# First two modulation vectors taken in four quarters of features, with the first three column blocks of the input projection fed from each quarter

## The chip, the cores and the metric

The kernel runs on one core of one Trainium2 chip. A core has five engines that run side by side and wait for each other through semaphores: TensorE (PE in the profile, its weight loads PEld), VectorE (DVE), ScalarE (ACT), GpSimd (POOL) and SyncE (SP). Here SP issues nearly all transfers; sixteen DMA engines carry them. The metric is the device time of one launch in microseconds.

## The reference, cut to what matters

Two transformer blocks over 256 tokens of 2048 features, all in float32. Only the start of the first block matters here. Six modulation vectors come from the condition `c`; the first two of them scale and shift the normalized input, and the result `h` is multiplied with `w_in` (2048 x 8192), whose columns are the state space input (1024), queries, keys and values (1024 each) and two gates (2048 each).

```python
mod = silu(c) @ w_ada[l] + b_ada[l]                 # 12288 values
sh1, sc1, g1, sh2, sc2, g2 = split(mod, 6)
h = rms_norm(x, norm_mix_g[l]) * (1.0 + sc1) + sh1  # 256 x 2048
z = h @ w_in[l]                                     # 256 x 8192
```

The state space branch takes the first 1024 columns of `z`. Before it can start it needs tables that depend only on its parameters (decay, angle, cosines and sines of 128 steps, block diagonal input and output operands). Attention with a relative position bias takes queries, keys and values. The merged branches, a feed forward, and a second block with its own mixer and an expert layer follow; none of that is touched.

## The kernel before

**Layout.** Activations lie feature major: 128 features on the partitions, 256 tokens along the row, 16 chunks for 2048 features. A product is taken with weights as the stationary operand (128x128) and a chunk of `h` as the moving one (128x256), summed in PSUM over the 16 chunks. For accuracy each operand is split in two parts, `hi` (rounded by ScalarE) and `lo` (the rest, by VectorE), and three products are summed: hi x hi, hi x lo, lo x hi. A block of 512 columns is 192 products in two PSUM banks.

**Weights.** `piece` loads 512 rows of 512 columns (1 MiB) into a tile `w` of pool tag W (4 buffers), ScalarE writes `wh` (tag H, 2 buffers) and VectorE `wl` (tag L, 2 buffers). `gemm` takes four pieces for one block; after each quarter of a piece's products it calls `bg`.

**Background work.** Everything that isn't on the main path is a Python generator in the list `work`. Each step issues some instructions and yields its VectorE time as the writer of the kernel reckoned it, the credit. `bg(dve, ada)` adds `dve` credits and issues steps, one generator after the other, until they are used up (at most 3 are carried over). `ada` moves the list `stream`, from which the later modulation vectors are fed, one 1 MiB tile a step. `drain` issues all that is left of a generator; `need` steps the stream until a vector is there.

**Order.** A scheduler puts the instructions in order at compile time, but while `pinned[0]` is true (from the start to just before the first `gemm`) each instruction of VectorE, ScalarE and TensorE is kept behind everything traced before it on its engine. SP's and GpSimd's are free.

**The head.** `ada_pe` takes one modulation vector on TensorE: 16 tiles `aw` of 128 rows by 2048 columns (1 MiB each, line 270), each in four products of a 128x32 operand `crep` (silu of `c`, repeated) with 128x512, into the four 32-partition strips of one PSUM tile `adap`: strip q holds feature columns 512q to 512q+511. `ada_fin` copies it (`adae`), transposes it (`adat`) and adds the bias. The call for vector (1, 1), the scale, is paced with `bg(2.5, 0)` a tile, that for (1, 0), the shift, with `bg(2.3, 0)`. Their tiles rotate over the tags W, H and L (`deep=True`). Under them run `x_in` (x transposed by TensorE into `xT`, its mean square, its row of factors `rstd`), `ssm_prep` (the state space tables: names `ex`, `ws`, `prm`, then `tab`, `ta`, `tb`, `el`, `q`, `e` in `ssm_table` and `ba`, `bb`, `bd`, `cd` in `ssm_blocks`), `columns` (small vectors, loaded by GpSimd as `rows`, transposed into `colT`), and `moba_bias`. `load_src` loads the state space sources `ssrc` by SP (lines 317 and 320). During the second vector `mod_scale` multiplies each chunk of `xT`; when it is there, `mod_shift` writes `h1h` on ScalarE and `h1l` on VectorE for all 16 chunks, and the first pieces of `w_in` are split. Then the blocks of `w_in` follow: two for `uT` (state space), two for `qT`, two for `kT`, and so on. `drain(g_ssm)` stands behind the first two blocks, and there the state space recurrence (`ssm`: names `bu`, `yp`) starts as background work; it must be through before the product with `w_glu`, whose operand is `zh`.

**Buffers.** Tag U of the pool `up` has 14 tiles of 1 MiB; the input x takes two, `h` four, `xT` two. PSUM has eight banks: three in the pool of `pacc_`, five in that of `pmisc`.

Of the kernel before, what the change touches and what calls it, by code (L numbers as in the profile page):

```python
# [20 lines left out]
P = 128  # L21
# [10 lines left out]
def _consts():  # L32
    """Tables that depend on the shapes alone."""
# [40 lines left out]
# Pacing: vector engine time (us) of background work and modulation tiles for each piece of weights.  # L74
# [5 lines left out]
def tile_kernel(ctx: ExitStack, tc: tile.TileContext, I, out):  # L80
# [3 lines left out]
    class Pinned:  # L84
        """An engine whose instructions keep their traced order while `pinned` is set."""
# [52 lines left out]
    # ---------------------------------------------------------------- constants  # L138
# [33 lines left out]
    # ---------------------------------------------------------------- background work  # L172
    # Generators that yield the vector engine time (us) of what they have just issued.
# [39 lines left out]
    # ---------------------------------------------------------------- modulation vectors  # L213
# [31 lines left out]
    def ada(blk, j, g=None):  # L245
        """One modulation vector, its products on the vector engine."""
# [17 lines left out]
    def ada_pe(blk, j, g, crep, pool=pmisc, deep=False):  # L264
        """One modulation vector, its products on the tensor engine."""
# [11 lines left out]

    packs = [
# [24 lines left out]
    # state space parameters, the first modulation vector, the relative position table  # L303
    for t in range(2):
        SY.dma_start(xtok[t], I["x"][0, t * P:(t + 1) * P, :])
# [6 lines left out]
    g_sc1 = ada_pe(1, 1, "norm_mix_g", crep, pacc_, True)  # L312
# [19 lines left out]
    # ---------------------------------------------------------------- norm pieces  # L332
    def rsqrt_of(ps, scale, w, r1=None):
        """(scale ps (r1^2) + eps) ** -0.5 of w columns."""
# [16 lines left out]
    def spread(cols, dst):  # L351
        """Columns of one value a token to rows over the tokens, the same on all partitions."""
        for i in range(len(cols)):
            dg = scr([P, P], "dg")
            S.activation(dg, ident, AF.Copy, scale=cols[i])
            T.matmul(dst[:, i * P:(i + 1) * P], ones, dg, start=True, stop=True, skip_group_check=True)
        return dst
# [5 lines left out]
    class Rms:  # L363
        """Mean square over the features of feature-major pairs, a value a token."""
# [26 lines left out]
    def residual(xs, gcol, c, b, quick=False):  # L391
        """x chunks c, c+1 += gate * product."""
# [11 lines left out]
    class HL:  # L404
# [18 lines left out]
        def put2(self, c, src):  # L423
            """Chunks c and c+1 of the operand from an f32 pair."""
# [23 lines left out]
    # ---------------------------------------------------------------- matrix products  # L448
# [10 lines left out]
    def gemm(w, kchunks, n0, segs, hl, kbase=0, dve=3.0, rate=0.5, pre=(), last=None):  # L459
        """Columns n0.. of h @ w.  segs: list of ('A' or 'B', columns, evac).  # L460
        A gives [128 features, token] tiles (two chunks a bank), B [token, feature] tiles."""
# [62 lines left out]
    # ------------------------------------------------ state space branch  # L524
    def exp_acc(x, shape, alloc):
        """(2^k, q) with exp(x) = 2^k (1 + q), by range reduction and a polynomial."""
# [95 lines left out]
    def ssm_table(cp2):  # L622
        """cos and sin of 0..127 times each state's angle, for one pair of chunks (8 state tiles)."""
# [29 lines left out]
    def ssm_blocks(cp2, src):  # L653
        """Block diagonal operands of one pair of chunks."""
# [125 lines left out]
    def moba_bias():  # L780
        """bias[q, h, col] = table at distance 128 + q - col, a skewed read of rows by distance."""
# [20 lines left out]
    # ================================================================ block 1  # L802
# [24 lines left out]
    g_x = start(x_in())  # L827
    g_ssm = start(ssm_prep())
    g_col = None
    for i, _ in enumerate(g_sc1):  # L830
        if i == 3:
            load_src()
        if i == 9:
            g_col = start(columns())
        if i == 6:
            start(moba_bias())
        if i == NC - 4:
            drain(g_x, g_col)
        bg(2.5, 0)
    rstd = r0[0]  # L840
    start(moba_flip())
    h = HL(16, "h1")
# [862 lines left out]
```

## Time and profile before

| | |
|---|---|
| three runs | 3382.13, 3378.8, 3382.21 us (median 3382.13) |
| the profiled execution, span from the first to the last instruction | 3379.9 us |
| TensorE busy (share of the span) | 2968.7 us (88%) |
| VectorE busy | 2300.7 us (68%) |
| ScalarE busy | 1024.1 us (30%) |
| GpSimd busy | 794.3 us (24%) |
| moved | 1068.18 MB, 316 GB/s in the mean |
| TensorE's share of the chain of work that ended last | 62% |

Of the profiled execution the span is the only time shown; no time of it around the span is given. A busy TensorE need not be at its peak: ends of matmuls are modelled, and a duration of a pipelined matmul is longer than the distance to the next one. The granted clock is given as a share of 2.4 GHz.

### The profile page before, as it was taken

What the parts mean: (1) busy time and instruction counts of PE and PEld (TensorE: products, weight loads), DVE (VectorE), ACT (ScalarE), POOL (GpSimd) and SP (SyncE); (2) the same over time, 40 slices, a digit from 0 to 9 for tenths busy, and PEclk for the clock granted to TensorE, in tenths of its full rate; (3) what the DMA queues carried; (4) which work ended last, traced back from release to release, by engine and by line L of the source; (5) the groups of instructions that cost most, each with busy time, mean ns of one, the idle gap of its engine ahead of it and who ended that gap; (6) DMA issues with size and microseconds to landing.
All of it is one profiled execution on the core that took longest, in us unless ns stands there. A gap on an engine that the chain in (4) does not pass through costs nothing.

```text
span 3379.9 us, 44134 instructions
## 1 busy us (share of the span) xinstructions
PE 2968.7 (88%) x18020; PEld 2299.5 (68%) x18020; DVE 2300.7 (68%) x3359; ACT 1024.1 (30%) x1360; POOL 794.3 (24%) x540
## 2 busy tenths in 40 slices
PE   6899999999999999999999999677876777667777
PEld 2687889999999999999999999333333333223233
DVE  7687779876778778865777668655655566664635
ACT  2323433444444444444347553111111101101100
POOL 1000000000000000000000003666665666665654
PEclk8899999999999999999999999898898889888888
DMA  9866667876899999864783447999999999999998
GB/s 368 301 220 214 202 234 248 305 266 217 295 328 337 320 322 325 324 238 166 259 276 102 138 150 291 418 421 422 421 421 422 422 421 422 421 421 409 422 374 355
DMA packets 278288, 1068.18 MB, mean 316 GB/s; under 512 B 27364, under 2 KB 31879, under 8 KB 187461
## 3 DMA queue, kind: packets, MB, share of 16 engines
q1 hardware_dynamic: 200258, 524.35, 44.3%
q0 software_dynamic: 74752, 538.26, 38.6%
q10 hardware_dynamic: 3076, 2.76, 0.3%
q8 instruction: 141, 2.31, 0.3%
q14 instruction: 61, 0.50, 0.0%
HBM read 1063.19 MB, written 2.11 MB: 315 GB/s over the span
## 4 chain that ended last, share of the span: by engine, by line
PE 62%; DMA 23%; issue 6%; DVE 4%; POOL 4%; ACT 1%; SPq 0%; POOLq 0%; DVEq 0%; ACTq 0%
PE ga L94 47%; DMA dn<-in_peer_down_dram,eid 12%; DMA up<-in_peer_up_dram,eid 9%; PE pe L94 6%; POOL dn L1599 2%; PE gb L94 2%; DMA aw<-in_w_ada_dram 2%; POOL up L1599 2%; PE adap L94 1%; DVE dn L94 1%; PE bu L94 1%; PE rms L94 1%; PE yp L94 1%; PE o L94 1%; PE cmp L94 0%
## 5 line engine op out<-in xcount | busy, mean ns | idle before, releaser
L94 PE MATMUL pe<-up,cdg 128*128 128x512 f32 x1936 | 914.4, 633 | 333.3 <-DMA up<-in_peer_up_dram,eid 202.3
L94 PEld LDWEIGHTS pe<-up,cdg 128*128 128x128 f32 x1936 | 387.7, 204 | 851.7 <-issue 636.7
L1599 POOL DMA_INDIRECT dn<-in_peer_down_dram,eid x256 | 397.7, 1554 | 2252.7 <-DVE rest L94 2003.0
L94 DVE TENSOR_TENSOR wl<-w,wh 128x2048 fp32r<-128x2048 f32 (+1 forms) x300 | 680.5, 2269 | 325.4 <-ACT wh L94 268.5
L94 ACT ACTIVATE wh<-w 128x2048 fp32r<-128x2048 f32 (+1 forms) x300 | 569.2, 1897 | 887.0 <-PE ga L94 715.4
L94 DVE SCALAR_TENSOR_TENSOR dn<-dn,htok 128x2048 f32<-128x2048 f32 x256 | 583.1, 2289 | 325.3 <-DMA dn<-in_peer_down_dram,eid 325.2
L1599 POOL DMA_INDIRECT up<-in_peer_up_dram,eid x256 | 383.6, 1499 | 276.1 <-PE pe L94 108.3
L94 DVE SCALAR_TENSOR_TENSOR acc<-aw,cT,acc 128x2048 f32<-128x2048 f32 x105 | 246.5, 2348 | 16.2 <-DMA aw<-in_ada_w_dram 10.2
L94 PE MATMUL ga<-h2h,wh 128*128 128x256 f32 x1024 | 250.1, 285 | 3.7 <-ACT h2h L94 3.7
L94 PE MATMUL ga<-h2l,wh 128*128 128x256 f32 x1024 | 249.6, 284 | 0.2 <-DVE h2l L94 0.2
L94 PE MATMUL ga<-ah,wh 128*128 128x256 f32 x1024 | 249.3, 283 | 0.0
L94 PE MATMUL ga<-al,wh 128*128 128x256 f32 x1024 | 249.0, 283 | 0.0
L94 ACT ACTIVATE cdg<-ca,cf 128x128 f32<-128x128 f32 x242 | 85.0, 394 | 488.9 <-PE pe L94 464.9
L94 PE MATMUL ga<-h1h,wh 128*128 128x256 f32 x896 | 224.0, 289 | 0.0
L94 PE MATMUL ga<-h1l,wh 128*128 128x256 f32 x896 | 220.4, 284 | 0.0
L94 PEld LDWEIGHTS ga<-h2h,wh 128*128 128x128 f32 x1024 | 197.3, 193 | 5.7 <-ACT h2h L94 4.0
L94 PEld LDWEIGHTS ga<-h2l,wh 128*128 128x128 f32 x1024 | 197.2, 193 | 0.5 <-DVE h2l L94 0.5
L94 PEld LDWEIGHTS ga<-ah,wh 128*128 128x128 f32 x1024 | 196.5, 192 | 0.8 <-ACT wh L94 0.8
L94 PEld LDWEIGHTS ga<-al,wh 128*128 128x128 f32 x1024 | 196.5, 192 | 0.0
L94 PEld LDWEIGHTS ga<-h1h,wh 128*128 128x128 f32 x896 | 172.7, 193 | 19.5 <-issue 15.3
L94 PEld LDWEIGHTS ga<-h1l,wh 128*128 128x128 f32 x896 | 172.9, 193 | 0.9 <-issue 0.8
L94 PE MATMUL ga<-h3h,wh 128*128 128x256 f32 x528 | 133.5, 291 | 1.1 <-ACT h3h L94 1.1
(443 smaller groups left out, 4581.4 us busy)
## 6 DMA issues: line engine op xcount, KB each, us to landing
w<-in_w_ff_dram SPq DMA_DIRECT2D x128, 1024.0 KB, 5.8
w<-in_w_in_dram SPq DMA_DIRECT2D x100, 1024.0 KB, 5.3
aw<-in_w_ada_dram SPq DMA_DIRECT2D x96, 1024.0 KB, 6.9
aw<-in_ada_w_dram SPq DMA_DIRECT2D x96, 1024.0 KB, 5.9
w<-in_w_out_dram SPq DMA_DIRECT2D x32, 1024.0 KB, 5.1
w<-in_peer_wq_dram SPq DMA_DIRECT2D x16, 1024.0 KB, 5.2
w<-in_w_proj_attn_dram SPq DMA_DIRECT2D x8, 1024.0 KB, 5.1
w<-in_w_proj_ssm_dram SPq DMA_DIRECT2D x8, 1024.0 KB, 6.2
```

Source lines behind the costliest of these rows:

```text
L94: r = f(*a, **k)
L1599: G.indirect_dma_start(out=rows_, out_offset=None, in_=table, in_offset=bass.IndirectOffsetOnAxis(ap=idx, axis=0))
```

## The change

The two first vectors are no longer taken whole, one after the other. `ada_quarter` takes 512 of a vector's 2048 features: four tiles of 512 rows by 512 columns (1 MiB each), the four strips now hold the four row chunks of a tile, and the finish sums over the strips. `first_mods(gi)` takes quarter gi of the scale and then of the shift, ten steps. The four chunks of `h` that a quarter gives are made at once, and `first_part` takes their products for the first three blocks of `w_in` (`uT` twice, `qT` once), whose six PSUM banks stay open over all four quarters: three of them from `pacc_`, three from `pmisc`. Within them, after each group of products, `advance` takes one step of the next quarter and 1.5 credits of background work. `x_in` and `columns` are issued during the first quarter, the load of x after two tiles; `load_src` and `ssm_prep` start at the second quarter, `moba_bias` at the third. All of this is still pinned. The three blocks leave PSUM after the fourth quarter; a fourth block follows as before, and the state space recurrence starts behind it.

```diff
+    def ada_quarter(blk, j, gi, dest, g):
+        ps = pmisc([P, 512], "adap")
+        sl = slice(4 * gi, 4 * gi + 4)
+        for k0 in range(0, NC, 4):
+            at[0] += 1
+            wt = wp.tile([P, 4, 512], F32, name=nm("aw"), tag="W") if at[0] % 2 else unit([P, 4, 512], "aw")
+            SY.dma_start(wt, adaw[blk][k0 * P:(k0 + 4) * P, j * D + 512 * gi:j * D + 512 * gi + 512]
+                         .rearrange("(c p) n -> p c n", p=P))
+            for q in range(4):
+                T.matmul(ps[32 * q:32 * q + 32, :], crep[:, k0 + q, :], wt[:, q, :],
+                         start=(k0 == 0), stop=(k0 == NC - 4), skip_group_check=True)
+            yield 0.0
+        ev = scr([P, 512], "adae")
+        S.copy(ev, ps)
+        pt = pmisc([P, 4, P], "adat")
+        for b in range(4):
+            T.transpose(pt[:, b, :], ev[:, 128 * b:128 * b + 128], ident)
+        V.tensor_reduce(dest[:, sl], pt.rearrange("p b (q r) -> p b q r", q=4)[:, :, :, 0], axis=AX.X, op=OP.add)
+        V.tensor_add(dest[:, sl], dest[:, sl], adab[blk][:, j * 16 + 4 * gi:j * 16 + 4 * gi + 4])
+        if g is not None:
+            V.scalar_tensor_tensor(dest[:, sl], dest[:, sl], 1.0, col[g][:, sl], op0=OP.add, op1=OP.mult)
+        yield 0.4
...
+    mods[(1, 1)], mods[(1, 0)] = (const([P, 16], "mod") for _ in range(2))
+
+    def first_mods(gi):
+        yield from ada_quarter(1, 1, gi, mods[(1, 1)], "norm_mix_g")
+        yield from ada_quarter(1, 0, gi, mods[(1, 0)], None)
+
+    def load_x():
+        for t in range(2):
+            SY.dma_start(xtok[t], I["x"][0, t * P:(t + 1) * P, :])
...
-    g_x = start(x_in())
-    g_ssm = start(ssm_prep())
-    g_col = None
-    for i, _ in enumerate(g_sc1):
-        if i == 3:
...
+    nfirst = 3
+    fb_ = [[(pacc_ if 2 * n + i < 3 else pmisc)([P, 2, L], "ga") for i in range(2)] for n in range(nfirst)]
+
+    def first_part(gi, n, hook):
+        whi, wlo = piece(w_in, 4 * gi, 4, 512 * n, 512)
+        for low in (False, True):
+            for i, b in enumerate(fb_[n]):
+                for kk in range(4):
+                    c = 4 * gi + kk
+                    for jj in range(2):
+                        sl = slice((2 * i + jj) * P, (2 * i + jj + 1) * P)
+                        if low:
+                            T.matmul(b[:, jj, :], wlo[:, kk, sl], h.hi(c), start=False, stop=(c == NC - 1),
+                                     skip_group_check=True)
+                        else:
+                            T.matmul(b[:, jj, :], whi[:, kk, sl], h.hi(c), start=(c == 0 and jj == 0), stop=False,
+                                     skip_group_check=True)
+                            T.matmul(b[:, jj, :], whi[:, kk, sl], h.lo(c), start=False, stop=False,
+                                     skip_group_check=True)
+                hook()
+
+    def advance(g, n=1, dve=1.5):
+        for _ in range(n):
+            next(g, None)
+        bg(dve, 0)
+
+    g = first_mods(0)
+    for k in range(10):
+        if k == 4:
+            drain(g_col)
+        if k == 2:
+            load_x()
+            g_x = start(x_in(), first=True)
+            g_col = start(columns(), first=True)
+        advance(g)
+    drain(g_x)
+    rstd = r0[0]
+    for gi in range(4):
+        for c in range(4 * gi, 4 * gi + 4):
+            mod_scale(xp, rstd, mods[(1, 1)], c, xp[c // 2][:, c % 2, :])
+            mod_shift(xp[c // 2][:, c % 2, :], mods[(1, 0)], c, h)
+        if gi == 1:
             load_src()
...
+            g_ssm = start(ssm_prep())
+        if gi == 2:
             start(moba_bias())
...
+        g = first_mods(gi + 1) if gi < 3 else iter(())
+        for n in range(nfirst):
+            first_part(gi, n, lambda: advance(g))
+        for _ in g:
+            pass
     start(moba_flip())
...
-    for nb in range(2):
-        gemm(w_in, NC, nb * 512, [("A", 512, store_pairs([uT], 4 * nb))], h, rate=TUNE["r1"], dve=TUNE["d1"], pre=pre if nb == 0 else ())
-
+    qT = unit([P, 8, L], "qT")
+    kT = unit([P, 8, L], "kT")
+    for n in range(nfirst):
+        ev = store_pairs([uT], 4 * n) if n < 2 else store_pairs([qT], 0, scale=SCALE)
+        for i in range(2):
+            ev(i, fb_[n][i])
+    gemm(w_in, NC, 1536, [("A", 512, store_pairs([qT], 4, scale=SCALE))], h, rate=TUNE["r1"], dve=TUNE["d1"])
     drain(g_ssm)
     g_ssm = start(ssm())
```

## Rows read from the trace of the kernel before

**Rows 1.** Busy time of each engine by stage; (x) is the count.
```profile
core 0: us, PE busy (x) PEld busy (x) DVE busy (x) ACT busy (x) POOL busy (x), PEclk, DMA share, GB/s
...
36.00:72.00 36.00, 28.08 (x130) 8.69 (x122) 31.35 (x146) 5.37 (x11) 1.45 (x2) 0.67 1.01 374
72.00:114.00 42.00, 29.22 (x154) 6.62 (x153) 36.90 (x167) 8.55 (x15) 0.00 (x0) 0.76 0.99 399
114.00:186.00 72.00, 72.00 (x555) 65.19 (x552) 41.39 (x52) 26.76 (x25) 0.00 (x0) 0.97 0.74 248
```

**Rows 2.** Chain of waits in order of time: start, duration (us), engine, tile, count.
```profile
98.59 13.43 DMA aw<-in_w_ada_dram
112.16 1.93 PE adap L94 x8
114.09 21.05 PE ga L94 x160
135.13 0.99 PE adap L94 x8
...
556.89 23.23 PE ga L94 x192
...
619.83 1.41 PE yp L94 x10
621.24 43.74 PE ga L94 x363
```

**Rows 3.** Timeline of ScalarE in the head: start, duration, instruction, count.
```profile
47.89 0.37 ACT L94 COPY rstd<-rows 128x256 f32<-128x256 f32 x1 [2.72 <-PE rows L94]
...
107.92 0.59 ACT L94 COPY adae<-adap 128x512 f32<-128x512 f32 x1 [22.92 <-PE adap L94]
109.46 1.70 ACT L94 ACTIVATE h1h<-xT,mod 128x256 fp32r<-128x256 f32 x4 [0.96 <-DVE mod L94]
...
114.47 1.89 ACT L94 ACTIVATE wh<-w 128x2048 fp32r<-128x2048 f32 x1
```

**Rows 4.** Timeline of TensorE in the head.
```profile
13.29 1.93 PE L94 MATMUL adap<-aw,crep 128*32 128x512 f32 x8 [7.28 <-DMA aw<-in_w_ada_dram]
...
19.26 1.07 PE L94 MATMUL adap<-aw,crep 128*32 128x512 f32 x8 [0.28 <-DMA aw<-in_w_ada_dram]
...
34.39 1.12 PE L94 MATMUL xt<-ca,xtok 128*128 128x128 f32 x4
```

**Rows 5.** Timeline of VectorE in the head.
```profile
16.91 0.15 DVE L94 TENSOR_SCALAR ex<-ld 32x2 f32<-32x2 f32 x1
...
34.63 0.30 DVE L94 COPY prm<-ptp 128x160 f32<-128x160 f32 x1
...
41.31 0.69 DVE L94 COPY xT<-xt 128x512 f32<-128x512 f32 x1 [0.37 <-PE xt L94]
...
64.70 0.48 DVE L94 MEMSET bd<- 128x512 f32 x1
...
68.25 0.48 DVE L94 MEMSET bd<- 128x512 f32 x1
...
90.02 0.16 DVE L94 COPY el<-prm 128x16 f32<-128x16 f32 x1
...
101.57 0.68 DVE L94 TENSOR_TENSOR ta<-tab,el 128x512 f32<-128x512 f32 x1
...
105.79 0.16 DVE L94 COPY el<-e 128x8 f32<-128x8 f32 x1
```

**Rows 6.** VectorE's groups, 12 to 114 us: busy us, mean ns; idle before.
```profile
L94 DVE SCALAR_TENSOR_TENSOR xT<-xT,mod,rstd 128x256 f32<-128x256 f32 x16 | 7.0, 480 | 0.0
...
L94 DVE COPY xT<-xt 128x512 f32<-128x512 f32 x8 | 5.4, 675 | 11.2 <-PE xt L94 11.2
...
L94 DVE TENSOR_TENSOR wl<-w,wh 128x2048 fp32r<-128x2048 f32 x1 | 2.3, 2291 | 1.3 <-DMA w<-in_w_in_dram 1.3
...
L94 DVE SCALAR_TENSOR_TENSOR h1l<-xT,mod,h1h 128x256 fp32r<-128x256 f32 x4 | 1.7, 483 | 0.6 <-ACT h1h L94 0.6
```

**Rows 7.** Timeline of the issuing queues of SP and GpSimd in the head.
```profile
19.24 15.94 SPq L317 DMA_DIRECT2D ssrc<-in_ssm_b_im_dram  x1
...
17.27 0.50 POOL L297 DMA_DIRECT2D rows<-in_k_norm_g_dram  x1 [0.29 <-DMA rows<-in_cmp_pe_k_dram]
```

More of the change, by code (lines that the diff above doesn't have):

```diff
@@ L276, in ada_pe @@
         yield 0.2
+    def ada_quarter(blk, j, gi, dest, g):
[20 more added lines that the diff above has]
+        yield 0.4
+    at = [0]
     packs = [
@@ L301, in tile_kernel @@
     adab.update({1: col["b_ada"], 2: col["ada_b_2"]})
-    for t in range(2):
-        SY.dma_start(xtok[t], I["x"][0, t * P:(t + 1) * P, :])
+    mods[(1, 1)], mods[(1, 0)] = (const([P, 16], "mod") for _ in range(2))
[5 more added lines that the diff above has]
+            SY.dma_start(xtok[t], I["x"][0, t * P:(t + 1) * P, :])
     ws = unit([P, 16, P], "ws")
@@ L311, in tile_kernel @@
     S.dma_start(ld, I["ssm_log_dt"][0].rearrange("(t g) -> t g", g=2))
-    g_sc1 = ada_pe(1, 1, "norm_mix_g", crep, pacc_, True)
     src = unit([P, 4, 512], "ssrc")
@@ L825, in x_in @@
         yield 0.1
-    g_x = start(x_in())
-    g_ssm = start(ssm_prep())
-    g_col = None
-    for i, _ in enumerate(g_sc1):
-        if i == 3:
+    g_x = None
+    h = HL(16, "h1")
+    w_in = I["w_in"][0]
+    nfirst = 3
[17 more added lines that the diff above has]
+                hook()
@@ L832, in tile_kernel @@
             load_src()
-        if i == 9:
-            g_col = start(columns())
-        if i == 6:
+            g_ssm = start(ssm_prep())
+        if gi == 2:
             start(moba_bias())
[L837 to L840, printed above, removed]
-    start(moba_flip())
-    h = HL(16, "h1")
-    for i, _ in enumerate(ada_pe(1, 0, None, crep, pacc_, True)):
-        if i < NC:
-            mod_scale(xp, rstd, mods[(1, 1)], i, xp[i // 2][:, i % 2, :])
-        bg(2.3, 0)
@@ L847, in tile_kernel @@
-    pre = []
-    for c in range(NC):
-        mod_shift(xp[c // 2][:, c % 2, :], mods[(1, 0)], c, h)
-        if c in (3, 7):
-            pre.append(piece(I["w_in"][0], c - 3, 4, 0, 512))
+        g = first_mods(gi + 1) if gi < 3 else iter(())
[3 more added lines that the diff above has]
+            pass
+    start(moba_flip())
     pinned[0] = False
@@ L863, in need @@
             cred[0] -= step(stream, False)
-    w_in = I["w_in"][0]
     for j, g_ in ((2, None), (4, "norm_mlp_g"), (3, None), (5, None)):
@@ L936, in moba @@
             yield 0.7
-    qT = unit([P, 8, L], "qT")
-    kT = unit([P, 8, L], "kT")
-    for nb in range(2):
-        gemm(w_in, NC, 1024 + nb * 512, [("A", 512, store_pairs([qT], 4 * nb, scale=SCALE))], h, rate=TUNE["r1"], dve=TUNE["d1"])
     for nb in range(2):
```

## The prediction

> **What bounds the kernel now.** I read the page's forty slices first: TensorE is busy in 9 of 10 from the second slice to the end of the first block's feed forward, so a gain can only come from the head. The busy times by stage [rows 1] show it: until 114.0 us TensorE has 29.2 of 42 us of work (at a mean clock of 0.76) and waits, while the 16 DMA engines run at 0.99 and 399 GB/s; from 114 to 186 us it is busy for all of 72 us and the DMA share falls to 0.74. VectorE is nearly full in the head too, 31.4 of 36 us and 36.9 of 42. The chain of waits says the same: aw transfers until 112, then products `ga` without a hole [rows 2]. 1 MiB at 399 GB/s is 2.6 us, and both vectors are 32 MiB. One block of 512 columns is 192 products in 23.23 us [rows 2], 0.121 us each; the first 160 take 21.05, 1.7 more than that, since they begin at the low clock.
>
> **The mark to beat.** The change moves work inside the head and leaves the number of products and their tiles alone. So I ask when TensorE is through with the first three blocks' 576 products if nothing else were mixed in. Before: 114.1 + 576 x 0.121 (69.7) + 1.7 = 185.5 us. What is mixed in there now (aw products of later vectors such as the 0.99 us at 135.13 [rows 2], `bu`, `yp`) falls to a later, TensorE-bound stage and cancels. The change gains 185.5 minus the same moment after.
>
> **Removed or unchanged.** The two vectors still move 32 MiB and take 128 matmuls; three blocks still take 12 MiB, 12 weight copies on ScalarE and 12 residues `wl` on VectorE. What goes is the deep rotation of aw over three pools and the two separate passes.
>
> **Added.** Eight finishes instead of two: each one ScalarE copy of 0.59 us [rows 3], four transposes (1.12 us at the low clock as in `xt` [rows 4]), and two or three small VectorE operations, 0.5 us in all. The new reduction of 128x4x4 from PSUM is not in the trace: between 0.16 (the 128x16 copy of `el`) and 0.30 us (the 128x160 copy to `prm`) [rows 5]; I take 0.2, as its input is small.
>
> **Moved: the first quarter.** x now follows two aw pieces, so it lands third and fourth where the first aw landed third, at 13.3 [rows 4]: about 16. Three of the five banks of the second PSUM pool are held by `ga`, one by `adap`: one is left for x's eight steps, each four transposes (1.12 [rows 4]) and then a copy (0.68 [rows 6]), in turn 1.8 us and 2 with hand-overs. Between them stand the four column transposes, and the last pack of rows is only issued at 17.27 [rows 7]; TensorE's order is pinned, so it waits. x is through at about 34. From the last x copy to the row of factors took 7 us (41.31 to 48.26) [rows 3, 5]: 41. Four groups of the second vector and its finish: 5 us. First modulation at 46. If x's copies overlapped, ten MiB of transfers and a finish would still be ahead: 13.3 + 7 x 2.6 + 2.5 = 34 at the least.
>
> At each hand-over the four chunks go scale on VectorE (0.48), shift on ScalarE (1.70/4), residue on VectorE (0.48) [rows 3, 6]. VectorE's order is pinned chunk by chunk, so this is a chain: 4 x 1.4 = 5.6, with hand-overs 5.8, and behind it the copy of the weights, 1.9. TensorE starts 7.7 us later. Then 144 products (17.4), eight aw pieces at 0.54 (4.3), transposes 1.1, slow start 1.7, last copy and sums 1.1, less the 16 products (1.9) that come after the last transposes: 31.4. So the second quarter is handed over at t1 = 46 + 31 = 77. The lower bound is 34 + 27 = 61, with no slow start and the modulation at its busy time.
>
> The upper bound, 88, is the state space source load: one of its issues held SP for 15.94 us [rows 7], and in the new order it stands ahead of the second quarter's first weights. By bandwidth there is room: 21 MiB are due by t1, 55 us of 77. I leave it hidden; without that cover it is 15.9 less two pieces still queued (5.2), 11 us.
>
> **Moved: the state space preparation.** It now starts at the second quarter. In the kernel before it ran on VectorE under the aw transfers from 16.91 on. Its price [rows 5]: parameters to the copy `prm`, 16.91 to 34.93, less four x copies of 0.6: 15.6. A block 64.70 to 68.25, 3.55, four of them: 14.2. A table 90.02 to 105.95, less three scales of 0.4 lying in it: 14.7, three of them 44.1, the last step of each 4.4. Sum 74. The hook after each group of products hands out 1.5 of the generator's own credit; its yields sum to 55, and the second quarter begins with 3 in hand. So the second quarter issues 21.8 credits (parameters and nearly one table, 30.0 us), the third 18.1 (blocks and most of a table, with the bias copy 0.7: 25.5), the last the remaining 15.2, about 15 us of it ahead of the last split. All of it stands in VectorE's pinned order in front of the next `wl`, which TensorE's low products need.
>
> VectorE's order, us: second quarter: chain 5.8, wait for the weight copy 1.9, three splits 6.9 (2.29 each [rows 6]), preparation 30.0, two finishes 1.0 and their waits 2.4: 48. Third: 5.8 + 1.9 + 6.9 + 25.5 + 3.4 = 43.5. Last: 5.8 + 1.9 + 6.9 + 15 and 16 low products 1.9: 31.5. Sum 123. With busy times alone (modulation 8 x 0.40, no waits) it is 41.1 + 36.6 + 27.0 = 104.7. The chain is real order, so I stand near the upper end and take off half of the finishes' waits and some of the weight copies': 119. TensorE needs at most 8 us a piece (48 products and four aw pieces), less than VectorE's 9 to 11, and the DMA 11 MiB x 2.6 = 29 us a quarter: neither sets it.
>
> So the three blocks end at 77 + 119 = 196 instead of 185.5: **10.5 us later.** VectorE stands nearly idle from about 10 to 77 us and then carries 74 us of preparation in line with the products that were to come early. The end points are 61 + 105 = 166 (19 earlier) and 88 + 123 = 211 (25 later).
>
> **Behind the head.** Twelve pieces with 3.6 credits and 0.65 steps of the stream are gone. The state space recurrence starts after the fourth block, with 14 blocks rather than 16 to hide in: by its credits it ended about one block before the end of the `sga` products, and its last `yp` at 621.2 had the rest of these in front of it (43.74 us of `ga` without a hole [rows 2]); now its last step falls due at their very end. The next product's first piece (48 x 0.121 = 5.8) covers most of what follows: 0 to 5 us, taken as 2. The stream reaches the feed forward eight steps later: at the need for vector 5 three steps are forced instead of none, 3 x 2.6 of DMA under pieces of 5.8 us of products each: 0 to 3, taken as 0.5.
>
> Sum: +13 on the profiled span of 3379.9; no other time of that execution is shown. The median of the runs is 3382.1, 2.2 above the span and within their own spread of 3.4. 3382.1 + 13 = **3395 us.** 0.2% (6.8 us) is about what a measurement can tell from no change.
>
> **Rivals.**
> A, the forecast: VectorE's pinned order sets the head; 3389 to 3408. For it: VectorE's shares of 0.87 and 0.88 in the old head [rows 1], with this same work under DMA waits.
> B, faster: the waits of the hand-over overlap, and the busy sum alone sets the pace. Place: the three hand-overs; price: 105 instead of 119, with t1 = 70: 175, that is 10 earlier, 3372, and 3363 with the earliest t1. It decides from an end of the third block before 179. For it: back to back operations at the rows shown; against it: the chunk-by-chunk order.
> C, no change: early products and late preparation cancel, end at 179 to 192.
> D, slower still: the clock. In the old head it averaged 0.67 and 0.76 [rows 1], and eight aw products took 1.93 us low and 1.07 high [rows 4]. At every hand-over TensorE now idles some 8 to 11 us. If it stayed at 1.2 GHz, a quarter costs 34.8 + 7.7 us of TensorE where 17.4 + 4.3 stand above: 21 more in the first, 4 to 11 in the others, 45 in all; a third of that is 15 on top of A: 3410. Against it: VectorE's slack lets TensorE catch up, and at 118 us it had come back to the high clock after some 4 us of products (the 1.7 us above).
> The Trainium skill's page "TensorE: Matmul & The Clock Gate" ("HAM oscillation — how this bites in real kernels") speaks for D: an array that waits between short bursts is throttled again, and every burst starts slow. By that rule the sum would be D's 3410; by the rows, with the slow start paid once in the first quarter, it is A's.
>
> **Chances.** A 0.50, B 0.20, C 0.20, D 0.10. Faster by over 0.2%: B, 0.20; within: C, 0.20; slower: A and D, 0.60. The range leaves out the lower half of B and the upper half of D, and holds the bounds of t1: 3369 to 3413; A's own is 3389 to 3408.
>
> **What will show it.** First `ga` near 54 us instead of 114; in the second to fourth quarter, pieces of 48 products with holes that end on `wl` or on VectorE's `tab`, `bd`, `ws`; VectorE over 0.9 busy from about 77 to 190 and under 0.4 before; the 576th product near 196 plus what is mixed in. Wrong would be: VectorE idle in those quarters while TensorE waits for aw or w (then DMA order sets it), a clock near 0.5 throughout (D), an end before 179 (B), or a hole of over 5 us at the first `zh` products.

## The result, and the profile after

The changed kernel takes 3463.7 us (median of four runs, 3462.1 to 3465.0) against 3381.7 (3378.8 to 3382.2): a ratio of 1.0241 with a 95% interval of 1.0228 to 1.0253, 82 us slower. The forecast was 13 us slower.

The busy times by stage of the changed kernel, cut at its four hand-overs (the first `h1h` of each quarter) and at the end of the three blocks, which answer to [rows 1]:

```profile
core 0: us, PE busy (x) PEld busy (x) DVE busy (x) ACT busy (x) POOL busy (x), PEclk, DMA share, GB/s
0.00:47.00 47.00, 22.25 (x113) 9.97 (x113) 9.38 (x32) 9.21 (x13) 11.48 (x26) 0.82 0.85 304
47.00:94.00 47.00, 31.06 (x210) 21.45 (x211) 11.25 (x17) 8.86 (x10) 0.00 (x0) 0.82 1.03 331
94.00:149.00 55.00, 33.68 (x229) 23.50 (x227) 38.63 (x150) 10.75 (x13) 0.00 (x0) 0.81 0.56 194
149.00:219.00 70.00, 39.63 (x254) 27.09 (x254) 34.73 (x132) 12.71 (x17) 1.46 (x2) 0.79 0.50 166
219.00:251.00 32.00, 25.03 (x188) 24.55 (x189) 27.49 (x88) 14.85 (x17) 0.00 (x0) 0.83 0.27 86
```

Read it line by line. The start is as forecast: the first hand-over comes at 47 (forecast 46). Then the quarters take 47, 55, 70 and 32 us, where the forecast had 31, 48, 43.5 and 31.5. In the 55 and the 70 nothing is full: VectorE works 38.6 and 34.7 us, near the busy sums of the forecast (41.1 and 36.6), but as a share that is 0.70 and 0.50; the DMA share is 0.56 and 0.50. In such a stage bandwidth and work do not set the time; what does is a chain of waits. The timeline of ScalarE at the first hand-over, which answers to [rows 3], shows the chain that was costed there:

```profile
47.14 0.51 ACT L94 ACTIVATE h1h<-xT,mod 128x256 fp32r<-128x256 f32 x1 [1.55 <-DVE xT L94]
48.59 0.51 ACT L94 ACTIVATE h1h<-xT,mod 128x256 fp32r<-128x256 f32 x1 [0.95 <-DVE xT L94]
50.05 0.51 ACT L94 ACTIVATE h1h<-xT,mod 128x256 fp32r<-128x256 f32 x1 [0.95 <-DVE xT L94]
51.51 0.51 ACT L94 ACTIVATE h1h<-xT,mod 128x256 fp32r<-128x256 f32 x1 [0.95 <-DVE xT L94]
51.92 3.69 ACT L94 ACTIVATE wh<-w 128x2048 fp32r<-128x2048 f32 x2
```

One chunk every 1.46 us (forecast 1.4), then the weight copy; the first `ga` product starts at 53.9 (forecast 54). What went wrong comes after it. TensorE's waits from 0 to 260 us (total, times, longest), in the changed kernel and, last, in the kernel before:

```profile
PE adap L94 <- DMA aw<-in_w_ada_dram: 48.1, 7, 9.5
PE ga L94 <- ACT wh L94: 40.2, 7, 11.7
```

```profile
PE adap L94 <- DMA aw<-in_w_ada_dram: 27.2, 13, 7.3
```

48 us are waits for aw tiles, 25.0 of them in the two stages in which the DMA share is 0.56 and 0.50. One of these waits, on TensorE and on the queue of SP (x8 is one tile: each of its four products gives two records):

```profile
164.92 1.07 PE L94 MATMUL adap<-aw,crep 128*32 128x512 f32 x8
...
167.66 1.19 PE L94 MATMUL ga<-h1h,wl 128*128 128x256 f32 x8
177.45 1.94 PE L94 MATMUL adap<-aw,crep 128*32 128x512 f32 x8 [8.59 <-DMA aw<-in_w_ada_dram]
```

```profile
137.94 22.30 SPq L285 DMA_DIRECT2D aw<-in_w_ada_dram  x3
166.05 0.37 SPq L483 DMA_DIRECT2D w<-in_w_in_dram  x1
166.47 0.50 SPq L285 DMA_DIRECT2D aw<-in_w_ada_dram  x1
172.69 15.78 SPq L483 DMA_DIRECT2D w<-in_w_in_dram  x2
```

The tile that TensorE takes at 177.45 is issued at 166.47, only 11 us before its use. What the DMA engines moved from 160 to 200 us, in 40 slices of 1 us:

```profile
GB/s 397 399 412 391 236 23 8 158 238 336 406 408 408 346 365 358 356 393 354 70 0 0 0 0 0 0 0 0 0 158 248 389 354 358 414 387 401 373 64 16
```

They stand idle from 165 to 167, just before that issue, and from 180 to 189, while SP holds for 15.78 us (172.69). What SP waited for from 47 to 219 us (total, times, longest) is buffers that other engines had still to free:

```profile
SPq L483 <- PE adap L94: 42.8, 5, 15.0
SPq L285 <- DVE wl L94: 26.8, 2, 19.0
```

Which tiles stand ahead of it is seen in the instruction order of the program (the numbers are the tiles' names; those that TensorE takes here are the eight of the last quarter, aw811 and aw895 are of the quarter before):

```
TensorE takes: aw1005  aw1042  aw1063  aw1108  aw1195  aw1220  aw1254  aw1293
SP issues:     aw1005  aw811  aw895  aw1063 | w1114 | aw1042  aw1195  aw1254 | w1271 | aw1108 | w1447  w1534 | aw1220  aw1293
```

aw1195 and aw1254 are taken after aw1108 and are issued before it; aw1042 and these two take 22.30 us (from 137.94), in which SP stands at one instruction until a buffer comes free. In the code the odd tiles of `ada_quarter` come from tag W, the even ones from the 14 buffers of tag U. TensorE's order is pinned; SP's is not, and the issues of the two tags are laid out apart from each other.

How far the delay goes through the kernel is read from the tiles' first and last times (us). The first row is the third block's second `qT` copy; for the kernel before it is the mark 185.5 of the prediction, which leaves out what is mixed in. The last three columns are versions of the experiments below.

| | before | changed | e5: SP in order | e9: pieces ahead too | e16: loop early, credit 4.1, rate 0.72 too |
|---|---|---|---|---|---|
| three blocks end | 185.5 | 251.3 | 203.9 | 193.2 | 191.1 |
| first `h2h` product | 820.1 | 887.0 | 839.6 | 832.0 | 828.0 |
| last `h2h` product | 1473.4 | 1547.0 | 1500.4 | 1491.7 | 1481.0 |
| first `h4h` product | 2001.1 | 2079.1 | 2032.5 | 2019.8 | 2011.3 |
| first `pe` product | 2136.8 | 2213.9 | 2167.5 | 2154.9 | 2146.5 |
| last `pe` product | 3372.5 | 3453.8 | 3400.2 | 3391.7 | 3386.2 |

Against that mark 66 of the 82 us are there when the three blocks end. The last stage, from the first `pe` to the last, takes 1233 to 1240 us in these kernels with no tie to the change, and single runs of one kernel spread by up to 5 us (the last experiment): differences below 5 us between single runs say nothing.

### The profile page after: what moved, and what is told of

Read it like the earlier page. It is cut to its first block, busy times and chain, and to the rows that moved or that the text cites. A ratio compares the mean times of both kernels' runs of the same rounds, so it can differ in the third digit from the quotient of the medians.

```text
span 3460.2 us, 44224 instructions
## 1 busy us (share of the span) xinstructions
PE 2983.2 (86%) x18044; PEld 2318.8 (67%) x18044; DVE 2306.3 (67%) x3376; ACT 1024.8 (30%) x1364; POOL 786.5 (23%) x540
## 5 line engine op out<-in xcount | busy, mean ns | idle before, releaser
L1661 POOL DMA_INDIRECT dn<-in_peer_down_dram,eid x256 | 380.7, 1487 | 2216.2 <-DVE rest L94 1961.7
L1661 POOL DMA_INDIRECT up<-in_peer_up_dram,eid x256 | 392.8, 1534 | 272.5 <-PE pe L94 107.9
L94 PE MATMUL ga<-h1h,wh 128*128 128x256 f32 x896 | 231.0, 295 | 40.2 <-ACT wh L94 40.2
L94 PEld LDWEIGHTS ga<-h1h,wh 128*128 128x128 f32 x896 | 177.0, 198 | 65.3 <-ACT wh L94 45.4
```

Source lines behind the costliest of these rows:

```text
L94: r = f(*a, **k)
L1661: G.indirect_dma_start(out=rows_, out_offset=None, in_=table, in_offset=bass.IndirectOffsetOnAxis(ap=idx, axis=0))
```

## The experiments

Each edit is to the changed kernel unless it says otherwise. All compute the same function. Where one time is given it is of one run; the kernel before took 3378 to 3383 us beside each.

**Whose buffers: one tag or the other.** The first theory was that the aw tiles which share the four buffers of tag W with the pieces of w hold the pieces up.

```diff
# e1_aw_units
-wt = wp.tile(..., tag="W") if at[0] % 2 else unit([P, 4, 512], "aw")
+wt = unit([P, 4, 512], "aw")
# e4_aw_w
+wt = wp.tile([P, 4, 512], F32, name=nm("aw"), tag="W")
```

> The changed kernel ran 81 us slower than the one before where 13 were forecast; its first quarter (from the first scale of a chunk to the first scale of the second quarter) took 46.7 us, the others 54.6, 70.7 and 25.5. Here every aw tile of the quarters comes from the 14 units of tag U, none from the four weight buffers of tag W; nothing else changes. Ring theory: the weight pieces and half of the aw tiles pass through the same four buffers in SP's order; a buffer comes free when VectorE's split or TensorE's aw products have passed, both pinned behind other work, so SP issues late and each late tile's landing stands in TensorE's order. Then the second and third quarter fall to some 48 and 45 us, and the run takes 3410 to 3435. Rival, VectorE's order: the preparation in VectorE's order alone makes the quarters long, and the buffers don't matter; the run stays within 10 us of 3463.

Measured: 3436.1 us, just above the theory's range; waits for aw 32.0 us.

> The dose the other way: every aw tile of the quarters passes through the four weight buffers of tag W. Ring theory: slower than the changed kernel by 20 us or more, with TensorE's waits for aw and wh growing. VectorE's order: no change beyond 5 us, since neither the preparation nor the order of VectorE changes.

Measured: 3423.5 us, waits for aw 10.9, for `wh` 47.5. The theory fell: more sharing is faster here, not slower. Either tag alone beats the two in turn. With tag W alone, aw and w come from one set of buffers and SP issues nearly all tiles in TensorE's order; with tag U alone the aw tiles are in order among themselves, and only the pieces of w are apart.

**The preparation taken out of the three blocks.**

```diff
# e2_prep_late
         if gi == 1:
             load_src()
-            g_ssm = start(ssm_prep())
...
     start(moba_flip())
+    g_ssm = start(ssm_prep())
     pinned[0] = False
```

> The state space preparation is started only behind the four quarters, outside the pinned order; the aw tiles still share the weight buffers. VectorE's order: the 74 us of preparation leave the second to fourth quarter, which fall to about 25 to 30 us each, TensorE no longer waits there for wh, and the three blocks end near 180; the preparation then comes due before the recurrence, which costs up to 30 us there; 3410 to 3440. Ring theory: with the splits of VectorE earlier the buffers come free earlier too, but SP still waits in its order for aw products of TensorE, and TensorE still waits 15 us or more for aw tiles behind 100 us; the quarters stay at 35 to 45 us; 3430 to 3455.

Measured: 3436.7 us. The three blocks end at 209.1, 42 us sooner, but 15 of these are given back: the state space loop starts later (its first sum 325 us against 288), and TensorE waits 7.8 us for its `p` at the end. The time lies in both ranges. So the preparation does stretch these quarters, but not to the point where nothing else is left: TensorE still waits 37.8 us for aw.

**The state space sources on GpSimd's queue.**

```diff
# e3_src_pool; e7_aw_w_pool: the same on e4_aw_w
-            SY.dma_start(src[:, k, :]...
+            G.dma_start(src[:, k, :]...
```

> The four loads of the state space sources are issued on GpSimd's queue instead of SP's, where they held the queue from 51.3 to 66.4 us in the first quarter. If the hold on SP is what made the first quarter 46.7 us instead of the forecast 31, it falls to about 31 to 36 and the run to 3446 to 3453. If the sources' small packets cost the DMA engines the same time from whichever queue, or TensorE waits there for the buffers anyway, the first quarter stays above 42 and the run within 5 us of 3463.

Measured: 3456.3 us, 7.4 less and between the two ranges; the first quarter takes 38 us in place of 47. On the changed kernel SP is held for 15 us (51.3 to 66.4) by these four loads, and 7 come through.

> All aw tiles from tag W, and the four ssrc loads issued by GpSimd in place of SP. Theory: the loads hold SP some 15 us at 37 to 52 us of the first quarter, and 7 to 10 us of it reach TensorE, as on the changed kernel (7.4 us there): 3413 to 3417 us, first quarter 34 to 37 us in place of 43. Rival (covered): with aw in order the hold is hidden behind the tiles already landed, 3421 to 3425 us.

Measured: 3424.0, no gain on 3423.5: the rival's time, but for another reason. In e3 GpSimd stood 18.6 us at the first of these loads, until an aw product had freed its buffer, and issued it at 35.5. Here, with no aw tile in tag U, nothing holds it: it issues the loads at 17 us, in the middle of the first modulation, whose last four tiles then arrive one by one. GpSimd and TensorE in this run:

```profile
17.37 1.74 POOL L349 DMA_DIRECT2D ssrc<-in_ssm_b_re_dram  x1
```

```profile
32.88 1.93 PE L94 MATMUL adap<-aw,crep 128*32 128x512 f32 x8 [0.77 <-DMA aw<-in_w_ada_dram]
35.29 1.94 PE L94 MATMUL adap<-aw,crep 128*32 128x512 f32 x8 [0.48 <-DMA aw<-in_w_ada_dram]
37.98 1.94 PE L94 MATMUL adap<-aw,crep 128*32 128x512 f32 x8 [0.76 <-DMA aw<-in_w_ada_dram]
40.92 1.93 PE L94 MATMUL adap<-aw,crep 128*32 128x512 f32 x8 [1.00 <-DMA aw<-in_w_ada_dram]
```

With SP issuing them (e4) the same products are one stretch of 5.24 us from 31.34 on. The first hand-over moves from 38.8 to 45.5. The Trainium skill, "Trainium Kernel Development and Optimization" (Key Constraints), says that loads issued by SP, ScalarE and GpSimd share the same 16 DMA engines, and that issuing from several saves only the issue time. These two runs agree with both halves: 7.4 us saved on the changed kernel, where the issue held SP, and on e4 no gain, since the same bytes then came ahead of the first hand-over.

**SP alone in program order.** The direct test of the order: tags, buffers and work stay, and SP's issues keep the traced order as the other engines' do.

```diff
# e5_sp_order
-    G, SY = nc.gpsimd, nc.sync
+    G, SY = nc.gpsimd, Pinned(nc.sync)
```

> Theory (order): in the changed kernel SP issues the weight loads out of step with the order in which TensorE takes them, because the tiles of the two tags U and W are handed out apart. Here the tags stay as they are, U and W in turn, and SP alone is kept in program order. If the order is the cost, TensorE's waits for aw in 0 to 260 us fall from 48 us to 15 or less and the time comes to 3415 to 3430 us, as with all tiles of one tag. Rival (the buffers): a tile of the U pool is what costs, since it holds up tables or operands of the preparation; then the time stays at 3450 to 3464 us and the waits for aw above 35 us.

Measured: 3408.6 us, **55 us less from this one line**, more than the 34 to 49 of the theory. Its waits of TensorE (0 to 260 us) and its busy times, cut at its own hand-overs:

```profile
PE ga L94 <- ACT wh L94: 41.4, 7, 12.2
PE adap L94 <- DMA aw<-in_w_ada_dram: 9.6, 3, 6.5
```

```profile
0.00:37.00 37.00, 18.20 (x113) 8.06 (x113) 9.24 (x32) 9.51 (x14) 11.52 (x26) 1.00 0.97 352
37.00:72.00 35.00, 28.57 (x211) 20.74 (x212) 11.24 (x16) 8.78 (x10) 0.00 (x0) 0.90 1.04 322
72.00:117.00 45.00, 32.16 (x228) 22.65 (x227) 38.40 (x150) 10.14 (x12) 0.00 (x0) 0.91 1.04 380
117.00:172.00 55.00, 38.37 (x254) 26.35 (x254) 35.12 (x133) 13.38 (x18) 1.46 (x2) 0.84 0.58 194
172.00:204.00 32.00, 25.54 (x189) 25.06 (x190) 27.79 (x87) 15.08 (x18) 0.00 (x0) 0.82 0.29 91
```

The same work and the same bytes: the waits for aw fall from 48.1 to 9.6 us, and the DMA share in the first three stages from 0.85, 1.03 and 0.56 to 0.97, 1.04 and 1.04. The DMA engines are now full until 117 us, and from 20 us on TensorE waits for no aw tile. The three blocks end 47 us sooner: 38.5 of waits for aw and 8.8 of TensorE's busy time.

e4 has the same order of issues as this run, tile for tile, but for the place of the sources, and all its aw tiles in the four buffers of tag W. It is 15 us slower. So the order is what the changed kernel pays most for, and the shared buffers of the first theory have a price too; how much of the 15 us is the place of the sources was not separated.

The 41.4 us for `wh` have more than one cause. Two of them, 12.2 and 11.7 us, stand at the third and fourth hand-over, where the copy is only the last of a row. VectorE there, from the last step of the shift to the first scaled chunk:

```profile
112.32 0.16 DVE L94 TENSOR_TENSOR mod<-mod,colT 128x4 f32<-128x4 f32 x1
...
116.69 0.48 DVE L94 SCALAR_TENSOR_TENSOR xT<-xT,mod,rstd 128x256 f32<-128x256 f32 x1
...
163.34 0.16 DVE L94 TENSOR_TENSOR mod<-mod,colT 128x4 f32<-128x4 f32 x1
...
171.22 0.48 DVE L94 SCALAR_TENSOR_TENSOR xT<-xT,mod,rstd 128x256 f32<-128x256 f32 x1
```

The vector is there, and 4.2 and 7.7 us of table steps of the preparation come first in VectorE's fixed order. The changed kernel and e16 have the same two gaps. No run moved these steps behind the scaling, so what that would give is open.

TensorE is busy 142.8 us up to the end of the three blocks here and 151.7 in the changed kernel (the sums of the two tables): the 9 us are the same products at a lower mean of the granted clock, 0.79 to 0.83 there and 0.82 to 1.00 here. A single hole shows its two levels, 1.2 and 2.4 GHz: behind the wait of 8.59 us above, one aw tile took 1.94 us, ahead of it 1.07. The Trainium skill's page that was weighed for rival D ("TensorE: Matmul & The Clock Gate", HAM oscillation — how this bites in real kernels) has an array that waits between short bursts throttled again; these rows agree. The 9 us are small beside the waits themselves.

**Pieces one ahead.** The copy `wh` and the residue `wl` of each piece are issued before the products of the piece in front of it, and the first piece of a quarter before its modulation.

```diff
# e6_ahead (on e4_aw_w), e9_order_ahead (on e5_sp_order)
     def first_part(gi, n, hook):
-        whi, wlo = piece(w_in, 4 * gi, 4, 512 * n, 512)
+        whi, wlo = nxt.pop(0)
+        if n + 1 < nfirst:
+            first_piece(gi, n + 1)
+        elif gi < 3:
+            first_piece(gi + 1, 0)
```

> All aw tiles from tag W (3423.5 us), and each piece of input weights is issued one piece ahead of its products, so that its copy by ScalarE and its subtraction by VectorE stand before the background work of the piece that runs. Theory (hand-over): TensorE's 47.5 us of waits for wh in 0 to 260 us come from the place of these copies in ScalarE's and VectorE's fixed order; they fall to 15 to 25 us and the time to 3390 to 3408 us. Rival (the modulation): the wait is for the shift and scale of a quarter, with the weight copy only named last; then the waits move to h1h and the time stays at 3416 to 3425 us.

Measured: 3408.5 us, 15 less than 3423.5 and at the edge of the theory's range. The waits for `wh` became 20.1 us for `h1h`, as the rival had it.

> SP in program order with the tags as in the changed kernel (3408.6 us), and pieces one ahead. Theory: TensorE's remaining 41 us of waits for wh in 0 to 260 us fall as they did with all tiles of tag W (47 us of wh became 20 us of h1h, and the time fell by 15): 3392 to 3402 us. Rival: with SP in order the weight copy is no longer what ends the wait, the modulation is, and nothing is gained: 3405 to 3411 us.

Measured: 3399.9 us, 8.7 less than 3408.6. Its waits:

```profile
PE ga L94 <- ACT h1h L94: 19.5, 6, 7.1
PE adap L94 <- DMA aw<-in_w_ada_dram: 11.1, 5, 6.4
```

The 41 us of waits for `wh` were in part the place of the copy in ScalarE's order; behind it stands the modulation, `h1h`, with 19.5 us (the table steps ahead of the scaling among its causes). Both the theory and its rival had a part of it.

> All aw tiles from tag W, pieces one ahead and ssrc by GpSimd together. If the three costs are apart and add, 3382 to 3402 us, near the kernel before (3378 to 3382). Rival (VectorE's preparation is a bound below which the three quarters cannot go, about 120 us from first to last hand-over): no lower than the better of the two alone, 3402 to 3412 us.

Measured: 3420.2 (tag W, pieces ahead and GpSimd together), 12 more than without GpSimd: the sources are issued at 16.5 us and the first hand-over comes at 48.8 instead of 42.5. The costs do not add, for a reason that neither expectation had.

**Behind the head.** With SP in order the three blocks end 18 us late and the whole 28. (The 11 us of the next expectation are taken later, at the last `sga` copy: 651.0 against 639.5.) Two edits of numbers, each of which moves VectorE's work:

```diff
# e10_order_rate (on e5_sp_order)
-TUNE = {"r1": 0.65,
+TUNE = {"r1": 0.78,
# e13_pace (on e9_order_ahead)
-"d1": 3.6
+"d1": 4.1
```

> SP in program order, and the rate of stream steps a piece in the products of the first block raised from 0.65 to 0.78, so that the eight steps that the first three blocks no longer give are made up later. With SP in order the head ends 11 us later than before and the whole 28, so 17 us go between 650 and 2170 us. Theory: 8 to 15 of these come from the vectors of modulation that run late (TensorE waiting for acc, more products of them at the end of the output projection): 3393 to 3401 us. Rival: they come from VectorE's work at the end of the state space branch and the rate changes nothing: 3405 to 3412 us.

Measured: 3428.9 us, 20 more than 3408.6. TensorE's largest wait from 260 to 1500 us:

```profile
PE yp L94 <- DVE p L94: 20.0, 2, 10.2
```

Neither range held, but the rival had the place: with more of the stream's products on VectorE the state space loop ends later still (last sum 685.4 against 663.0 in e5). That loop is the thing that is late, as its sums on VectorE show (count; ns; first to last start), in the kernel before, in e9 and in e13:

```profile
L94 DVE TENSOR_TENSOR p<-p,p x32: 681/686/696, 183.1 to 613.6; 128x512 f32<-128x512 f32 x32
```

```profile
L94 DVE TENSOR_TENSOR p<-p,p x32: 679/684/693, 234.1 to 656.3; 128x512 f32<-128x512 f32 x32
```

```profile
L94 DVE TENSOR_TENSOR p<-p,p x32: 681/684/689, 234.8 to 599.4; 128x512 f32<-128x512 f32 x32
```

> SP in program order and pieces one ahead (3399.9 us), with the credit of VectorE's background work a piece raised from 3.6 to 4.1 in the products behind the head. There VectorE's state space loop ends 43 us later than before (last product 656 against 614) and TensorE waits for it 5 us at its end. Theory: the 17 to 19 us lost behind the head are the state space loop's late end; with the higher credit it ends near 615 and the time falls by 5 to 12 us, 3388 to 3395. Rival: the loss is the modulation vectors that run late, and the time stays at 3397 to 3403.

Measured: 3397.5. The loop ends 57 us sooner, TensorE's waits at its end (`yp`, `zhh`, `zhl`, 4.9 us) are gone and the first `h2h` product comes at 825.8 instead of 832.0. The stage behind it still takes 660 us against 653 before (820.1 to 1473.4), and the last stage was 3 us longer in this run, so that the total shows only 2.5. The early end is the theory's, the time the rival's.

```diff
# e14_ssm_first (on e9_order_ahead), e15_ssm_pace (also d1 4.1), e16_ssm_pace_rate (also r1 0.72)
+    g_ssm = start(prep_then_ssm(g_ssm))    # the loop behind the preparation, one generator
     gemm(w_in, NC, 1536, ...)
-    drain(g_ssm)
-    g_ssm = start(ssm())
```

> As that (3399.9 us), but the state space loop may start within the fourth block's products, behind the preparation, in place of behind the block. Theory of the late state space loop: it starts 20 to 30 us sooner, the 5 us at its end go, and the time falls by 5 to 10 us: 3390 to 3395. Rival as above: 3397 to 3403.

Measured: 3393.2, within the theory's range; first `h2h` at 826.6.

> Both together. If the loop's end is covered by one of them, no better than the better of the two (3388 to 3394); VectorE's work moved forward may also delay the weight subtractions (wl) of the blocks, by which the time would rise above 3400.

Measured: 3399.2, between the two ranges: no better than one alone.

> Both together, and the rate of stream steps 0.72 in place of 0.65. With the state space loop no longer last, the steps that the first three blocks no longer give can be made up: TensorE's wait for acc (4 us) and the products at the end of the output projection come back, 3380 to 3390 us. If VectorE is full there, as the rate of 0.78 alone showed (20 us of waits for the loop's p), 3400 to 3412 us.

Measured: 3395.2, between the two ranges; first to last `h2h` 653.0 us, as before the change, and no wait for `acc` any more. With the loop early, the late modulation vectors are made up without the 20 us of waits of e10; the rate was 0.72 here and 0.78 there, so the two causes are not apart. The times of e9 and of e13 to e16 lie within 7 us, little more than the spread of one kernel: what is shown here are the stages, not the totals.

**The preparation earlier.** All on SP in program order, with the sources on GpSimd's queue.

```diff
# e11_order_early (on e5); e12_all (pieces ahead and r1 0.78 too)
+    g_ssm = start(ssm_prep())              # ahead of the first modulation, 2.2 of credit a tile
     for k in range(10):
# e17_prep_q0 (on e16)
-        if gi == 1:
+        if gi == 0:
             load_src()
             g_ssm = start(ssm_prep())
# e18_prep_early (on e16): started at k == 4 of the first modulation, credit 1.2
```

> SP in program order; the preparation is started with the first product of the first modulation, where VectorE is idle, its sources loaded by GpSimd. Theory: VectorE's preparation is what stretches the second and third quarter; with its parameters and first table done by 36 us the three blocks end 15 to 25 us sooner: 3385 to 3396 us. Rival: the preparation stands in front of the first modulation's small VectorE operations and of x, and only changes place: first hand-over later by 5 to 10 us and the time 3403 to 3415 us.

Measured: 3412.2, first hand-over 51.0 in place of 36.7: the rival, with a larger delay than it had.

> SP in program order, pieces one ahead, preparation early, rate 0.78 together. If the three are apart and add: 3360 to 3380 us, at or below the kernel before. If they share one cover (TensorE bound by the loads of the quarters, 8 tiles of 1 MiB and three pieces): no lower than 3385 us.

Measured: 3422.8; first hand-over 57.3. The three blocks end at 197.2 (193.2 in e9), and from there to the first `h2h` (857.2) the kernel loses 21 us on e9, as e10 with the same rate loses 20 on e5.

> SP in program order, pieces one ahead, state space loop in the fourth block with credit 4.1, rate 0.72 (3395.2 us), and the preparation started one quarter earlier, behind the first modulation, its sources loaded by GpSimd. If VectorE's preparation is what stretches the second and third quarter (45 and 48 us there against 33 in the first), these shrink by more than the first grows, and the time falls by 8 to 15 us to 3380 to 3387, level with the kernel before. If the quarters are bound by TensorE's own hand-over chain and loads, only the order changes: 3392 to 3400.

Measured: 3404.6 us (four runs), ratio to the kernel before 1.0067 (1.0051 to 1.0084). Above both ranges: the third quarter shrinks as the theory had it, from 47.9 to 39.0 us, but the second stays (46.0 to 47.2), the first grows from 32.1 to 45.4, and the first hand-over goes from 41.2 to 48.8.

> The same with the preparation's parameters started within the first modulation at a small credit (1.2 a tile), where the earlier start at a larger credit had put tables in front of the norm's factor and the first hand-over 14 us later. If the parameters (15.6 us of VectorE) go into VectorE's idle time before the first hand-over, 3375 to 3385 us; if they delay the first hand-over again, it comes later than 42 us and the time is 3388 to 3400.

Measured: 3400.4 us (3397.0 to 3402.3), ratio 1.0058 (1.0041 to 1.0075); first hand-over 51.2. In all four runs the sources go out at 16 to 17 us, as in e7, so their late first hand-over is not VectorE's doing alone; what an early preparation costs by itself was not separated.

## Why the prediction was wrong, step by step

**Right.** The direction; the chain at the hand-over (1.46 us a chunk for 1.4), VectorE's busy time in the second and third quarter (38.6 and 34.7 for 41.1 and 36.6) and the last quarter (32 for 31.5).

**Right by luck.** The first hand-over at 47 (46), and with it the first product at 53.9 (54). The forecast had x set it; in the run x's last transposes stood behind an aw tile for which TensorE waited 7.92 us, until 33.79, and with SP in order the same hand-over comes at 36.7. The end of the three blocks near the forecast 196, once SP is in order (203.9, and 193.2 with the pieces ahead), is no better: it is a first hand-over 9 us early (36.7 for 46) and a longer way behind it (167 us for 150).

**The step that failed** is the sentence "TensorE needs at most 8 us a piece (48 products and four aw pieces), less than VectorE's 9 to 11, and the DMA 11 MiB x 2.6 = 29 us a quarter: neither sets it." It counted the transfers by their bandwidth. The rows of the changed kernel show them half idle from 94 to 219 us and TensorE waiting 48 us for them in the head: what counts is when each transfer is issued, and SP issued tiles of two tags in an order other than the one in which TensorE takes them. e5 changes that order alone and takes 55 of the 82 us away; e4, by another way (one tag), takes 40. The prediction named the sign of this itself ("VectorE idle in those quarters while TensorE waits for aw or w"), but among the things that would make it wrong, with no price and no chance.

**Mis-sized.** The same sentence and the first quarter's sum count an aw tile's products at 0.54 us, half of what they take: the trace has eight records a tile (256 for the 32 tiles), 1.07 us at the higher clock. The first quarter is then 35.7 us instead of 31.4, and with SP in order it took 35; TensorE's fullest piece is 10.1 us instead of 8, no longer below VectorE's 9 to 11. The source load, left hidden, came through with 7 us of its 11 "without that cover" on the changed kernel (e3). The cost behind the head was set at 2.5: it is 4.9 us of waits at the loop's end and 6.7 from the first to the last `h2h` product by way of the late vectors (653.3 to 660.0), as e13 and e16 show by taking each away.

**The rivals.** D, the clock, was real and small: 9 us of TensorE's busy time between the changed kernel and e5, whose own clock is not full either. B and C fell. A's cause, VectorE's pinned order, is partly borne out: taking the preparation away ends the three blocks 42 us sooner (e2), and at the third and fourth hand-over its table steps stand in front of the scaling. Yet VectorE is busy at most 0.87 of a quarter (27.8 of 32 in the last with SP in order), where over 0.9 was forecast.

**Open.** What is left after all repairs: e16 ends the three blocks at 191.1, 5.6 us behind the mark, and the kernel is 14 us slower than before in one run. Of its head, TensorE waits 20 us for `h1h` and 12 for aw. The table steps ahead of the scaling (4.2 and 7.7 us) are a part of the first that the trace shows and no run took away; whether the transfers (share 1.04 to 117 us in e5) would set the head next was not separated, since the early preparations moved the sources as well. With SP in order the third quarter still takes 54.5 us, 11 more than forecast, and 48.3 with the pieces ahead. The kernel before was not run with SP in order. No version here beats the kernel before; e14, the fastest, took 3393.2.

## What to carry to other kernels

When one queue issues loads for a consumer with a fixed order, count not only bytes by bandwidth but the order of the issues: in this kernel tiles taken in turn from two pools became free at different times, and an issue that stood waiting for its buffer held all behind it, the urgent one too. One pool for such a stream, or the issuing queue pinned to the consumer's order, is a one-line test, and a stage with no engine and no transfer full is a sign to make it. And where a paced generator starts late, giving it more credit or an earlier start brought its end back (e13, e14), while making other work on the same engine faster pushed it further out (e10).

## What the runs showed of the hardware that was not expected

Loading the same 1 MiB of sources from another queue was worth 7.4 us in one kernel and nothing in the next (e3, e7): issued at 35.5 us it freed SP, issued at 17.4 us it ran among the tiles of the first modulation, and the first hand-over came 7 us later. And 1 MiB of aw landed 9.7 us (median, 0 to 262 us) after its issue in the changed kernel and 10.6 with SP in order, against 2.6 us by bandwidth: the time from issue to landing did not fall, and still the waits for aw fell from 48.1 to 9.6 us, because the tiles were issued in the order of their use. The late tile above was issued 11 us before TensorE took it.
